# Two layer norms on transposed activations: folding the partial sums on VectorE before the float32 products

## The chip, the cores and the metric

The kernel runs on one core of a Trainium2 chip. The metric is device time of one launch, in microseconds (us). All inputs come from HBM and all outputs go back to it.

## The reference

One inference step of a single-layer encoder on 576 tokens (512 of a prompt, 64 of a sample). The part around the change is the end of the layer:

```python
def layer_norm(x, g, b):
    mu = mean(x, axis=-1);  var = mean(square(x - mu), axis=-1)
    return (x - mu) * rsqrt(var + LN_EPS) * g + b

def finish_layer(x, mix, pe, ...):
    x = layer_norm(ALPHA * x + mix @ w_o, ln1_g, ln1_b)
    hid = square(relu(x @ w_up))                          # 1024 -> 4096
    x = layer_norm(ALPHA * x + hid @ w_down, ln2_g, ln2_b)
    return x + sigmoid(x @ w_ple_gate + b_ple_gate) * (pe @ w_ple)
```

Before it stand a projection of `x` and two kinds of attention, whose outputs make `mix`. Everything is float32.

## The kernel before

Activations lie transposed: the 1024 features are 8 tiles of 128 partitions, the tokens are the columns. `Y` (128 x 8 x 576) holds the residual. The large products split each operand into a high and a low half in a reduced float32 type and make three TensorE products of each pair (`gemm`, L278). The weights are split on the way: ScalarE casts the high half (`whl<-wraw`, L182), VectorE subtracts it for the low half (L186), and SyncE loads the next raw tile into one of a few slots (L163).

A layer norm therefore needs sums over partitions, which TensorE makes with a matrix of 1/1024 (`onesm`). These products are in full float32. The class `LayerNorm` works on one half of the columns: the first norm on A and B of 288 columns each (`L1A`, `L1B`), the second on `A2` of 256 and `B2` of 320 (`L2A`, `L2B`). For each half:

- `add(j)` is called when feature tiles j and j+1 are final. It sums the tiles pairwise into `ln_s` (128 x 2 x w), on VectorE for half A and on GpSimd for the others, the last one (j = 6) always on VectorE (L1103, L1105). After it `ln_s` holds two rows of partial sums.
- `steps()` makes the mean with two products, one for each of the two rows (L1127). It then subtracts the mean on VectorE (L1131), squares on ScalarE (L1133, L1136) and sums the squares, again into two rows (L1137, on VectorE for A and for the last pair, else on GpSimd). The variance comes out of products with `ln_s` as the weights and one column of `onesm`, in blocks of up to 128 tokens, again twice per block (L1145): three blocks for 288 and 320 columns, two for 256. ScalarE takes the root (L1150), VectorE the reciprocal (L1151), and TensorE transposes it back (L64) for the scaling on VectorE (L1160). The high and low halves go to `BH` (ScalarE, L1164) and `BL` (VectorE, L1168).

The first norm runs beside the last two feature tiles of the attention output (`wo2`, whose results VectorE adds to `Y` at L1211) and beside the product with `w_ple` (`ple`, products `g<-pT`, whose results ScalarE copies to `PL` at L1224). Here three PSUM buffers named `g` go round, so that a product group waits until the group three places earlier has been taken out. The second norm runs beside the last `w_down` products (`down_last`, VectorE adds them at L1386) and beside the `w_ple_gate` products.

`drive` walks through a main generator and interleaves the norm's steps with it; `later` puts evictions a step behind. The framework that builds the program may then move an instruction past others of its engine, so that an edit can change the order around it, too. Apart from the sums GpSimd does nothing in this part.

Of the kernel before, what the change touches and what calls it, by code (L numbers as in the profile page):

```python
# [11 lines left out]
OP = mybir.AluOpType  # L12
# [23 lines left out]
def tile_hybrid_step(ctx: ExitStack, tc: tile.TileContext, I, O):  # L36
    nc = tc.nc
    PE, ACT, DVE, POOL, SP = nc.tensor, nc.scalar, nc.vector, nc.gpsimd, nc.sync
# [4 lines left out]
    def f(ap):  # L43
        return ap.bitcast(F32)
# [7 lines left out]
    onesm = base.tile([128, 128], F32, name="onesm")  # L52
# [10 lines left out]
    def transpose(out, in_, n):  # L63
        PE.transpose(out, in_, ident[:n, :n])  # L64
# [58 lines left out]
    class Weights:  # L123
# [9 lines left out]
        def add(self, ap, pool_l=False, pair=None):  # L133
            aps = [ap] if pair is None else [ap, pair]
            n = 2 if pair is None else 7
            self.items.append(dict(aps=aps, h0=self.nh, n=n, pool=pool_l, left=None, when=0))
            self.nh += n
            return len(self.items) - 1
# [941 lines left out]
    def psum_n():  # L1080
        return psN.tile([128, 512], F32, name="n", tag="n", bufs=2)
# [3 lines left out]
    class LayerNorm:  # L1085
# [10 lines left out]
        def add(self, j):  # L1096

            y = Y[:, :, self.sl]
            self.sums = j
            if j == 0:  # L1100
                self.s = fb.tile([128, 2, 320], F32, name="ln_s", tag="ln_s" if self.sl.start else "relu", bufs=1 if self.sl.start else 2)[:, :, :self.w]
            elif j == 2:
                (DVE if self.sl is A else POOL).tensor_tensor(self.s, y[:, 0:2], y[:, 2:4], OP.add)  # L1103
            else:
                (DVE if j == 6 or self.sl is A else POOL).tensor_tensor(self.s, self.s, y[:, j:j + 2], OP.add)  # L1105

        def pump(self):
            return next(self.gen, 0)
# [9 lines left out]
        def steps(self):  # L1118
            sl, gi, w = self.sl, self.gi, self.w
            y = Y[:, :, sl]  # L1120
            while self.sums < 6:
                yield 1
            for _ in range(self.waits[0]):
                yield 1
            mu = psum_n()[:, :w]
            for x in range(2):
                PE.matmul(mu, onesm, self.s[:, x], start=(x == 0), stop=(x == 1))  # L1127
            mb = mu[:, None, :].to_broadcast([128, 2, w])
            ss = self.s
            for j in range(0, 8, 2):  # L1130
                DVE.tensor_tensor(y[:, j:j + 2], y[:, j:j + 2], mb, OP.subtract)  # L1131
                if j == 0:
                    ACT.activation(ss, y[:, 0:2], AF.Square)  # L1133
                else:
                    sq = fb.tile([128, 2, 320], F32, name="ln_sq", bufs=2)[:, :, :w]
                    ACT.activation(sq, y[:, j:j + 2], AF.Square)  # L1136
                    (DVE if j == 6 or sl is A else POOL).tensor_tensor(ss, ss, sq, OP.add)  # L1137
                yield 1
            for _ in range(self.waits[1]):
                yield 1  # L1140
            blks = [(c, min(128, w - c)) for c in range(0, w, 128)]
            var = psum_n()
            for i, (c, n) in enumerate(blks):
                for x in range(2):
                    PE.matmul(var[:n, i:i + 1], ss[:, x, c:c + n], onesm[:, 0:1], start=(x == 0), stop=(x == 1))  # L1145
            rt = fb.tile([128, 4], F32, name="ln_r", bufs=2)
            for i, (c, n) in enumerate(blks):
                if i == 0 or n < 128:
                    m = len(blks) - (blks[-1][1] < 128) if i == 0 else i + 1
                    ACT.activation(rt[:n, i:m], var[:n, i:m], AF.Sqrt, bias=epst[:n, 0:1])  # L1150
                    DVE.reciprocal(rt[:n, i:m], rt[:n, i:m])  # L1151
            for _ in range(self.waits[2]):
                yield 1
            rb = psum_n()[:, :w]
            for i, (c, n) in enumerate(blks):
                transpose(rb[:, c:c + n], rt[:n, i:i + 1].to_broadcast([n, 128]), n)

            def scale(j):
                for x in (j, j + 1):
                    DVE.scalar_tensor_tensor(y[:, x], y[:, x], gb[:, gi, x:x + 1], rb, op0=OP.mult, op1=OP.mult)  # L1160

            def high(j):
                for x in (j, j + 1):
                    ACT.activation(BH[:, x, sl], y[:, x], AF.Identity, bias=gb[:, gi + 1, x:x + 1])  # L1164

            def low(j):
                for x in (j, j + 1):
                    DVE.scalar_tensor_tensor(BL[:, x, sl], y[:, x], gb[:, gi + 1, x:x + 1], f(BH[:, x, sl]),  # L1168
                                             op0=OP.add, op1=OP.subtract)
                self.ready += 1  # L1170

            def bias(j):
                for x in (j, j + 1):
                    ACT.activation(y[:, x], y[:, x], AF.Identity, bias=gb[:, gi + 1, x:x + 1])

            scale(0)
            high(0)
            yield 1
            scale(2)
            high(2)  # L1180
            low(0)
            yield 1
            for j in (4, 6):
                scale(j)
                high(j)
                yield 1
                low(j - 2)
                yield 1
            low(6)
            yield 1  # L1190
            for _ in range(self.waits[3]):
                yield 1
            for j in range(0, 8, 2):
                bias(j)
                yield 1

    def wo2(hs, ln, steps):
        for j in range(0, 8, 2):
            m = psum_g()
            for x in range(2):  # L1200
                cs = slice((j + x) * 128, (j + x + 1) * 128)
                for k in (6, 7):
                    W = unit_w(U["ok", k], U["ok", 6])
                    for _ in gemm(m[:, x, :HW], W, (0,), BH[:, k:k + 1], BL[:, k:k + 1], hs,
                                  first=(k == 6), last=(k == 7), wc=cs):
                        pass
                WT.step(steps)
                yield 1

            def ev(j=j, m=m):  # L1210
                DVE.tensor_tensor(Y[:, j:j + 2, hs], m[:, :, :HW], Y[:, j:j + 2, hs], OP.add)  # L1211
                ln.add(j)
            later(0, ev)
# [95 lines left out]
    def up_sums(g):  # L1309
# [4 lines left out]
        def pair(m):  # L1314
            h0 = WT.items[U["P", g, m]]["h0"]
            r = fs.tile([128, 4, HW], F32, name="r", bufs=2)
            u = fs.tile([128, 3, HW], F32, name="u")
            tt = DVE.tensor_tensor

            steps = ((x11, lambda ps: ACT.copy(u[:, 0], ps)),  # L1320
                     (x12, lambda ps: tt(r[:, 0], ps, u[:, 0], OP.add)),
                     (SX[2], lambda ps: tt(u[:, 1], ps, u[:, 0], OP.add)),  # L1322
                     (SX[3], lambda ps: tt(u[:, 2], ps, u[:, 1], OP.add)),
                     (x22, lambda ps: tt(r[:, 1], ps, u[:, 2], OP.add)),
                     (SX[1], lambda ps: (tt(r[:, 3], ps, u[:, 2], OP.subtract), tt(r[:, 2], ps, u[:, 1], OP.subtract))),
                     (SX[4], lambda ps: tt(r[:, 2], ps, r[:, 2], OP.add)))
            oh, ol = [hid[g][:, x, 2 * m:2 * m + 2].rearrange("p a (b t) -> p (a b) t", b=2) for x in range(2)]
            for i, (x, fn) in enumerate(steps):
                if i % 2 == 0:
                    G = psum_n()[:, None] if i == 6 else psum_g()  # L1330
                ps = G[:, i % 2, :HW]
                hv = WT.half(h0 + i)
                for _ in gemm(ps, lambda part, kw, wc, hv=hv: hv[part][:, kw, wc], range(4), x[0], x[1], slice(0, HW)):
                    WT.step()
                    yield 1
                later(0, lambda fn=fn, ps=ps: fn(ps))
                if i in (4, 6):
                    z = slice(i - 4, i - 2)
                    later(0, lambda z=z: ACT.activation(r[:, z], r[:, z], AF.Relu))
                    later(0, lambda z=z: ACT.activation(r[:, z], r[:, z], AF.Square))  # L1340
                    later(0, lambda z=z: ACT.copy(oh[:, z], r[:, z]))
                    later(0, lambda z=z: tt(ol[:, z], r[:, z], f(oh[:, z]), OP.subtract))
# [213 lines left out]
```

## Time and profile before

| | before |
|---|---|
| time, median of 3 runs | 803.52 us (803.4 to 804.11) |
| profiled execution, span | 802.3 us |
| median above the span | 1.2 us |
| TensorE busy | 788.6 us (98%) |
| VectorE, ScalarE, GpSimd busy | 537.9, 430.5, 118.2 us |
| mean products (L1127) | 16 records |
| variance products (L1145) | 44 records |

The page gives the span of the profiled execution and no other time of it. One float32 product shows as two records, a split product (L278) as one. PE is TensorE, PEld its weight loads, DVE is VectorE, ACT ScalarE, POOL GpSimd, SP SyncE. In a timeline a row gives the start in us, the length of the merged run, the engine, line and operation, the count, and in brackets the idle time before it with what ended it. In the chain, a row gives start, length and what the chain went through.

### The profile page before, as it was taken

The numbers are of one execution on the slowest core, as the hardware profiler recorded it, in microseconds if no ns is written. First come the engines' busy times: TensorE is split into PE (matmuls) and PEld (weight loads), VectorE is DVE, ScalarE is ACT, GpSimd is POOL, SyncE is SP. The second block draws the span as 40 slices with busy tenths as digits, with TensorE's granted clock in tenths as the row PEclk, the third lists the DMA queues.
The fourth block names the chain that finished last, engine by engine and source line by source line (L and its number), as shares of the span: only waits on it lengthen the run. The fifth ranks groups of instructions, "written<-read, shape, count | busy, mean of one in ns | idle before, by whom it ended". The sixth has DMA issues, their size and how long they took to land.

```text
span 802.3 us, 14965 instructions
## 1 busy us (share of the span) xinstructions
PE 788.6 (98%) x5916; PEld 760.0 (95%) x5916; DVE 537.9 (67%) x1092; ACT 430.5 (54%) x904; POOL 118.2 (15%) x117
## 2 busy tenths in 40 slices
PE   7999999999999999999999999999999999999997
PEld 7988898999999999999999999999999999999997
DVE  6679999644456555989755758577594765647553
ACT  5468656787677544497424427154362634626351
POOL 7202344354241000110000000000000000012200
PEclk9999999999999999999999999999999999999999
DMA  8537143254222223442213313142231413720001
GB/s 278 184 42 165 59 111 96 86 183 141 85 86 85 70 81 123 152 152 72 87 53 107 105 53 110 49 132 80 79 106 31 154 54 105 249 106 27 27 28 66
DMA packets 30358, 81.44 MB, mean 102 GB/s; under 512 B 5072, under 2 KB 9168, under 8 KB 30160
## 3 DMA queue, kind: packets, MB, share of 16 engines
q1 hardware_dynamic: 30288, 80.49, 32.3%
q8 instruction: 46, 0.75, 0.4%
q14 instruction: 24, 0.20, 0.1%
HBM read 66.38 MB, written 9.54 MB: 95 GB/s over the span
## 4 chain that ended last, share of the span: by engine, by line
PE 86%; DVE 8%; ACT 2%; DMA 1%; issue 1%; POOL 0%; SPq 0%; DVEq 0%; ACTq 0%
PE g L278 54%; PE m L278 18%; PE n L278 2%; DVE dbias L637 2%; PE V L909 2%; PE T L64 2%; DVE m L635 2%; PE S L822 1%; PE S L423 1%; PE S L820 1%; PE m L416 1%; PE m L423 1%; PE X L64 1%; DVE whl L186 1%; DVE dbias L615 1%
## 5 line engine op out<-in xcount | busy, mean ns | idle before, releaser
L182 ACT CAST whl<-wraw 128x512 fp32r<-128x512 f32 (+1 forms) x226 | 134.9, 611 | 173.4 <-PE g L278 145.6
L278 PE MATMUL g<-BH,whl 128*128 128x288 f32 (+2 forms) x864 | 181.8, 298 | 0.1
L278 PE MATMUL m<-AH,whl 128*128 128x288 f32 x736 | 178.3, 309 | 0.0
L186 DVE TENSOR_TENSOR whl<-wraw,whl 128x512 fp32r<-128x512 f32 (+1 forms) x192 | 129.9, 695 | 69.2 <-ACT whl L182 68.3
L278 PEld LDWEIGHTS g<-BH,whl 128*128 128x128 f32 x864 | 141.2, 188 | 2.3 <-ACT u L1320 1.2
L278 PEld LDWEIGHTS m<-AH,whl 128*128 128x128 f32 x736 | 126.4, 188 | 3.7 <-issue 2.2
L278 PE MATMUL g<-BL,whl 128*128 128x288 f32 (+2 forms) x432 | 127.4, 295 | 0.0
L278 PE MATMUL m<-AL,whl 128*128 128x288 f32 x368 | 109.2, 297 | 0.0
L278 PE MATMUL g<-hidE,whl 128*128 128x288 f32 (+2 forms) x768 | 103.4, 295 | 0.0
L278 PE MATMUL g<-hidO,whl 128*128 128x288 f32 (+2 forms) x768 | 103.3, 295 | 0.0
L278 PEld LDWEIGHTS g<-hidO,whl 128*128 128x128 f32 x768 | 102.3, 188 | 0.0
L278 PEld LDWEIGHTS g<-hidE,whl 128*128 128x128 f32 x768 | 102.2, 188 | 0.1
L278 PEld LDWEIGHTS g<-BL,whl 128*128 128x128 f32 x432 | 81.4, 188 | 0.1
L278 PEld LDWEIGHTS m<-AL,whl 128*128 128x128 f32 x368 | 69.6, 189 | 0.5
L278 PE MATMUL g<-s,whl 128*128 128x288 f32 x432 | 68.5, 298 | 0.0
L278 PEld LDWEIGHTS g<-s,whl 128*128 128x128 f32 x432 | 60.1, 188 | 2.2 <-DVE u L1322 1.1
L838 ACT ACTIVATE sP<-sP,st 128x128 f32<-128x128 f32 (+4 forms) x72 | 39.6, 551 | 40.6 <-DVE st L830 40.2
L1103 POOL TENSOR_TENSOR ln_s<-Y 128x576 f32<-128x576 f32 (+2 forms) x3 | 4.6, 1550 | 383.7 <-DVE Y L1386 371.3
L186 POOL TENSOR_TENSOR whl<-wraw,whl 128x512 fp32r<-128x512 f32 x34 | 44.1, 1297 | 86.8 <-ACT whl L182 68.9
L1361 DVE SCALAR_TENSOR_TENSOR Y<-Y,g 128x576 f32<-128x576 f32 x48 | 36.0, 750 | 21.6 <-PE g L278 21.2
L278 PE MATMUL m<-BH,whl 128*128 128x288 f32 x192 | 43.5, 304 | 0.0
L278 PEld LDWEIGHTS m<-BH,whl 128*128 128x128 f32 x192 | 32.1, 188 | 0.8 <-issue 0.5
(278 smaller groups left out, 1243.2 us busy)
## 6 DMA issues: line engine op xcount, KB each, us to landing
wraw<-in_w_up_dram SPq DMA_DIRECT2D x32, 512.0 KB, 3.5
wraw<-in_w_down_dram SPq DMA_DIRECT2D x32, 512.0 KB, 3.5
wraw<-in_w_qkv_dram SPq DMA_DIRECT2D x23, 512.0 KB, 3.8
wraw<-in_w_gate_dram SPq DMA_DIRECT2D x8, 512.0 KB, 5.0
wraw<-in_w_o_dram SPq DMA_DIRECT2D x8, 384.0 KB, 3.1
out_vT_dram<-v SPq DMA_DIRECT2D x8, 288.0 KB, 2.1
Y<-in_xT_dram SPq DMA_DIRECT2D x8, 288.0 KB, 5.6
PLD<-PL SPq DMA_DIRECT2D x4, 576.0 KB, 2.8
```

Of the source, the lines that this page charges most:

```text
L64: PE.transpose(out, in_, ident[:n, :n])
L182: ACT.copy(self.hv[h][0], src)
L186: eng.tensor_tensor(lv, src, f(hv), OP.subtract)
L278: PE.matmul(ps, W(w, kw, wc), a[:, ka, cols], start=(first and i == 0), stop=(last and i == n - 1))
L416: PE.matmul(mk[:, h, :HW], w0(part, k), a[:, k, h * HW:(h + 1) * HW], start=(k == 0 and i == 0), stop=(k == 7 and i == 2))
L423: PE.matmul(acc[b][:n[b], :304], a[:, k, b * 128:b * 128 + n[b]], ixw(part, k), start=(k == 0 and i == 0), stop=(k == 7 and i == 2))
L615: DVE.scalar_tensor_tensor(dst[:n, :nk], r[:n, :nk], w, dst[:n, :nk], op0=OP.mult, op1=OP.add)
L635: DVE.max(m, s)
L637: DVE.match_replace(out=s, in_to_replace=m, in_values=s, imm_value=GONE)
L838: ACT.activation(j["P"], j["P"], AF.Exp, bias=j["st"][:, 0:1], scale=-1.0, accum_out=s)
L909: PE.matmul(P["O"][r, (i - 1) * 128 + c.start:(i + 1) * 128], P["vt"][:, kb, r], j["PT"][:, hh, kb, c], start=(kb == 0), stop=(kb == i))
L1361: later(0, lambda y=y, m=m, s=s: DVE.scalar_tensor_tensor(y, y, s, m[:, :, :HW], op0=OP.mult, op1=OP.add))
```

## The change

The two rows of partial sums are added into the first by one more VectorE instruction (128 x w), once after the last `add` and once after the last sum of squares. The mean then takes one product and the variance one per block, so that each of the four pairs of the mean and the eleven pairs of the variance loses one product, 15 in all.

```diff
@@ class LayerNorm, add
                 (DVE if j == 6 or self.sl is A else POOL).tensor_tensor(self.s, self.s, y[:, j:j + 2], OP.add)
+            if j == 6:
+                DVE.tensor_tensor(self.s[:, 0], self.s[:, 0], self.s[:, 1], OP.add)
@@ steps
             mu = psum_n()[:, :w]
-            for x in range(2):
-                PE.matmul(mu, onesm, self.s[:, x], start=(x == 0), stop=(x == 1))
+            PE.matmul(mu, onesm, self.s[:, 0], start=True, stop=True)
...
                     (DVE if j == 6 or sl is A else POOL).tensor_tensor(ss, ss, sq, OP.add)
+                if j == 6:
+                    DVE.tensor_tensor(ss[:, 0], ss[:, 0], ss[:, 1], OP.add)
                 yield 1
...
             for i, (c, n) in enumerate(blks):
-                for x in range(2):
-                    PE.matmul(var[:n, i:i + 1], ss[:, x, c:c + n], onesm[:, 0:1], start=(x == 0), stop=(x == 1))
+                PE.matmul(var[:n, i:i + 1], ss[:, 0, c:c + n], onesm[:, 0:1], start=True, stop=True)
```

In the changed kernel the new additions are L1107 (sum) and L1140 (squares); L1128 is the mean, L1147 the variance, L1132 the subtraction, L1138 the sum of squares, L1213 the addition of `wo2`, L1226 the copy to `PL`. In the second norm the built program has the same order as before with the new instructions put in. In the first norm three engines run in another order.

VectorE, from the addition of tiles 2 and 3 of half B (`Y<-g,Y`) on; before:

```order
L1211 TENSOR_TENSOR Y<-g,Y 128x2x288
L186 TENSOR_TENSOR whl<-wraw,whl 128x512
L1131 TENSOR_TENSOR Y<-Y,n 128x2x288 x2
L1211 TENSOR_TENSOR Y<-g,Y 128x2x288
L1131 TENSOR_TENSOR Y<-Y,n 128x2x288
L1137 TENSOR_TENSOR ln_s<-ln_s,ln_sq 128x2x288
L1131 TENSOR_TENSOR Y<-Y,n 128x2x288
L1137 TENSOR_TENSOR ln_s<-ln_s,ln_sq 128x2x288
L1211 TENSOR_TENSOR Y<-g,Y 128x2x288
L1137 TENSOR_TENSOR ln_s<-ln_s,ln_sq 128x2x288
L1105 TENSOR_TENSOR ln_s<-ln_s,Y 128x2x288
```

The same stretch of VectorE in the changed kernel:

```order
L1213 TENSOR_TENSOR Y<-g,Y 128x2x288
L1107 TENSOR_TENSOR ln_s<-ln_s 128x288
L186 TENSOR_TENSOR whl<-wraw,whl 128x512
L1213 TENSOR_TENSOR Y<-g,Y 128x2x288
L1132 TENSOR_TENSOR Y<-Y,n 128x2x288 x4
L1138 TENSOR_TENSOR ln_s<-ln_s,ln_sq 128x2x288
L1213 TENSOR_TENSOR Y<-g,Y 128x2x288
L1138 TENSOR_TENSOR ln_s<-ln_s,ln_sq 128x2x288
L1105 TENSOR_TENSOR ln_s<-ln_s,Y 128x2x288
L1138 TENSOR_TENSOR ln_s<-ln_s,ln_sq 128x2x288
L1107 TENSOR_TENSOR ln_s<-ln_s 128x288
L1140 TENSOR_TENSOR ln_s<-ln_s 128x288
```

The four subtractions now stand in one block behind the third `Y<-g,Y` of half B, and the fourth comes behind one sum of squares where two stood before.

ScalarE over the squares of half A; before (with what each instruction waits for):

```order
L182 CAST whl<-wraw 128x512 [waits DMAHW1_49,PE_49]
L1133 ACTIVATE ln_s<-Y 128x2x288 [waits DVE_49]
L1136 ACTIVATE ln_sq<-Y 128x2x288 [waits DVE_49]
L182 CAST whl<-wraw 128x512 [waits PE_49]
L182 CAST whl<-wraw 128x512 [waits DMAHW2_49,PE_49]
L1136 ACTIVATE ln_sq<-Y 128x2x288 [waits DVE_49]
L1224 COPY PL<-g 128x576 [waits PE_49]
```

The same stretch of ScalarE in the changed kernel:

```order
L182 CAST whl<-wraw 128x512 [waits PE_49]
L1134 ACTIVATE ln_s<-Y 128x2x288 [waits DVE_49]
L182 CAST whl<-wraw 128x512 [waits DMAHW2_49,PE_49]
L1137 ACTIVATE ln_sq<-Y 128x2x288 [waits DVE_49] x2
L1226 COPY PL<-g 128x576 [waits PE_49]
```

A weight cast moved ahead of the first square; the first copy to `PL` stays behind the two squares into `ln_sq`.

TensorE at the second mean, after the first 12 `g<-pT` products; before:

```order
L278 MATMUL g<-pT,whl 128x288 [waits DVE_49]
L278 MATMUL g<-pT,whl 128x288 x11
L278 MATMUL g<-pT,whl 128x288 [waits Activation_49]
L278 MATMUL g<-pT,whl 128x288 x2
L278 MATMUL g<-pT,whl 128x288 [waits DVE_49]
L278 MATMUL g<-pT,whl 128x288 x9
L1127 MATMUL n<-ln_s,onesm 128x288 [waits DVE_49]
L1127 MATMUL n<-ln_s,onesm 128x288
```

The same stretch of TensorE in the changed kernel:

```order
L278 MATMUL g<-pT,whl 128x288 [waits DVE_49]
L278 MATMUL g<-pT,whl 128x288 x11
L278 MATMUL g<-pT,whl 128x288 [waits Activation_49]
L278 MATMUL g<-pT,whl 128x288 x4
L278 MATMUL g<-pT,whl 128x288 [waits DVE_49]
L278 MATMUL g<-pT,whl 128x288 x16
L1128 MATMUL n<-ln_s,onesm 128x288 [waits DVE_49]
L1147 MATMUL n<-onesm,ln_s 128x1 [waits DVE_49]
```

The second mean (half B) stands nine split products later than before, with the first variance (half A) right behind it. The first mean, too, stands eight split products later than before, in the last group of `wo2`. The second variance keeps its place behind the last `g<-pT` product, and the second set of transposes stands 46 split products behind it where 42 stood.

On SyncE the second of two `w_up` loads now comes behind three stores of `PL` instead of ahead of them.

## The prediction

> **What bounds the kernel now.** I read the page first (busy shares, then the chain that ended last), then the chain cut to the two norms, then the waits and the timelines of each engine there.
>
> ```profile
> span 802.3 us, 14965 instructions
> PE 788.6 (98%) x5916; PEld 760.0 (95%) x5916; DVE 537.9 (67%) x1092; ACT 430.5 (54%) x904; POOL 118.2 (15%) x117
> PE 86%; DVE 8%; ACT 2%; DMA 1%; issue 1%; POOL 0%; SPq 0%; DVEq 0%; ACTq 0%
> ```
>
> TensorE is the bound: what leaves its queue leaves the time, unless a wait takes its place. The chain in the first norm (300 to 350 us) and the second (715 to 765 us) has every product group that the change halves:
>
> ```profile
> 327.57 0.99 PE n L1127 x4
> 336.52 0.98 PE n L1127 x4
> 337.77 1.00 PE n L1145 x12
> 347.52 1.00 PE n L1145 x12
> 718.02 0.86 PE n L1127 x4
> 731.21 0.79 PE n L1145 x8
> 748.76 1.08 PE n L1127 x4
> 760.59 1.11 PE n L1145 x12
> ```
>
> All eight lie on the chain. Together they are 0.99 + 0.98 + 0.86 + 1.08 = 3.91 us for the mean and 1.00 + 1.00 + 0.79 + 1.11 = 3.90 us for the variance.
>
> The two norms differ in what stands beside them. Busy time by stretch, then VectorE and GpSimd in the first norm:
>
> ```profile
> 318.00:330.00 12.00, 11.86 (x85) 11.20 (x84) 11.93 (x20) 5.92 (x10) 1.78 (x1) 1.00 0.57 190
> 327.17 0.75 DVE L1211 TENSOR_TENSOR Y<-g,Y 128x576 f32<-128x576 f32 x1
> 327.83 0.68 DVE L186 TENSOR_TENSOR whl<-wraw,whl 128x512 fp32r<-128x512 f32 x1
> 328.58 1.42 DVE L1131 TENSOR_TENSOR Y<-Y,n 128x576 f32<-128x576 f32 x2
> 331.25 1.63 DVE L1137 TENSOR_TENSOR ln_s<-ln_s,ln_sq 128x576 f32<-128x576 f32 x1
> 334.13 0.74 DVE L1211 TENSOR_TENSOR Y<-g,Y 128x576 f32<-128x576 f32 x1
> 328.05 1.78 POOL L1103 TENSOR_TENSOR ln_s<-Y 128x576 f32<-128x576 f32 x1 [12.39 <-DVE Y L1211]
> 330.81 1.45 POOL L1105 TENSOR_TENSOR ln_s<-ln_s,Y 128x576 f32<-128x576 f32 x1 [0.98 <-DVE Y L1211]
> ```
>
> In the first row VectorE (fourth figure) is busy 11.93 of 12.00 us, while TensorE (second figure) is busy 11.86. So in the first norm two engines are full, and an instruction added to VectorE is not free there.
>
> **The products removed.** Is half of the records half of the time? The mean of 256, 288 and 320 columns takes 0.86, 0.99 and 1.08 us, which is 3.36, 3.44 and 3.38 ns per column: the time goes with the columns and has no fixed part that would stay. The variance takes 0.79 / 8 = 0.099 us per record of a full block. So the saving is 3.91 / 2 = 1.95 us and 3.90 / 2 = 1.95 us: 1.92 us of the sum in the second norm, 1.98 us in the first. From below, a switch that stays at 0.1 us for each of the eight groups would leave 3.1 us; I take 3.9 because of the three widths.
>
> **The additions, second norm.** Four additions, of 256 and 320 columns. Their cover:
>
> ```profile
> 714.46 0.69 DVE L1105 TENSOR_TENSOR ln_s<-ln_s,Y 128x512 f32<-128x512 f32 x1
> 724.08 0.69 DVE L1137 TENSOR_TENSOR ln_s<-ln_s,ln_sq 128x512 f32<-128x512 f32 x1 [1.20 <-POOL ln_s L1137]
> 745.37 0.83 DVE L1105 TENSOR_TENSOR ln_s<-ln_s,Y 128x640 f32<-128x640 f32 x1
> 755.59 0.83 DVE L1137 TENSOR_TENSOR ln_s<-ln_s,ln_sq 128x640 f32<-128x640 f32 x1 [2.70 <-POOL ln_s L1137]
> ```
>
> The sums end at 715.15, 724.8, 746.2 and 756.4; by the chain rows the products that need them take their turn at 718.02, 731.21, 748.76 and 760.59. The smallest distance is 2.6 us. An addition there costs at most 0.83 us (the row of twice its width), so all four are covered by queued split products, even if TensorE comes 0.4 to 1.4 us earlier. Behind them on VectorE wait weight halves and, last, the gate's output for half A2; VectorE has idle time in brackets in two of these rows, so nothing late reaches TensorE. Cost 0; second norm -1.92 us.
>
> **The additions, first norm.** Four additions of 128x288 from SBUF, a form that the trace does not have. Neighbours:
>
> ```profile
> 351.47 3.07 DVE L186 TENSOR_TENSOR whl<-wraw,whl 128x512 fp32r<-128x512 f32 x5
> L1326 DVE TENSOR_TENSOR r<-n,r x12: 448/452/458, 439.2 to 691.6; 128x288 f32<-128x288 f32 x12
> ```
>
> Back to back, 576 columns are spaced 0.66 us (327.17 to 327.83) and 512 columns (3.07 - 0.68) / 4 = 0.60 us, about 1.04 ns per column; that puts 288 columns at 0.37 us of queue. The other end is the full length of 0.45 us with one operand in PSUM. I take 0.37, since the queue is packed there. The Trainium skill, VectorE: DVE Perf Modes, section "The DRAIN you can't avoid", says that the next op does not start before the pipe is empty, which would charge the full length; here L186 starts at 327.83, 0.09 us before the L1211 in front of it ends, so the trace disagrees. By the rule the four would take 1.8 us instead of 1.5 us.
>
> More costly is whom the first addition lets in. It stands at 327.83 in front of the weight half L186 that stood there, and GpSimd asks for its sum at 328.05:
>
> ```profile
> 721.02 3.03 POOL L1137 TENSOR_TENSOR ln_s<-ln_s,ln_sq 128x512 f32<-128x512 f32 x2 [8.11 <-ACT ln_sq L1136]
> 721.48 1.40 DVE L186 TENSOR_TENSOR whl<-wraw,whl 128x512 fp32r<-128x512 f32 x1
> ```
>
> A VectorE addition with both operands in SBUF that meets a running GpSimd sum takes 1.40 instead of 0.69 us and ends after it (also 331.25: 1.63 us instead of 0.75), while the subtraction at 328.58, with one operand in PSUM, ran at normal speed beside the sum at 328.05. The Trainium skill, SBUF — State Buffer, section "SBUF: two separate sides", calls this an exclusive lock that goes to whichever starts first, for its whole instruction; these rows agree, and who gets it between two VectorE instructions in a row the rule leaves open (rival b).
>
> Before, L186 was first and GpSimd waited (1.78 against 1.45 us). Now the addition ends at 328.20, GpSimd runs to about 329.65, and L186 goes with it to about 330.1, 1.6 us later than before. The queue then runs: third `Y<-g,Y` to 330.8, four subtractions to 333.4, one sum of squares to 334.1, fourth `Y<-g,Y` to 334.8. ScalarE follows the subtractions: square, cast, two squares to 333.85, first copy to `PL` to 334.4. TensorE waits for these:
>
> ```profile
> 327.40 1.14 PE L1127 MATMUL n<-ln_s,onesm 128*128 128x288 f32 x4
> 330.79 3.74 PE L278 MATMUL g<-pT,whl 128*128 128x288 f32 x27
> 334.93 1.59 PE L278 MATMUL g<-pT,whl 128*128 128x288 f32 x10 [0.40 <-DVE Y L1211]
> 332.58 0.64 ACT L1224 COPY PL<-g 128x576 f32<-128x576 f32 x1 [0.24 <-PE g L278]
> 344.64 0.76 DVE L1137 TENSOR_TENSOR ln_s<-ln_s,ln_sq 128x576 f32<-128x576 f32 x1 [1.89 <-POOL ln_s L1137]
> 345.66 1.86 PE L278 MATMUL g<-pT,whl 128*128 128x288 f32 x12 [0.15 <-ACT PL L1224]
> 351.33 0.20 DVE L1151 RECIPROCAL ln_r<-ln_r 128x2 f32<-128x2 f32 x2
> 354.25 0.39 PE n L64 x3
> ```
>
> One split product takes (3.74 - 0.29) / 26 = 0.133 us. In my working the mean starts at 327.40 + 8 x 0.133 = 328.47 (its addition is done by 328.2) and takes 0.49; the `g<-pT` products start at 330.29. After 24 of them, at 333.47, the next group needs the buffer that the first `PL` copy frees at 334.4: a wait of about 1.0 us, where before 0.55 us passed between 334.38 and 334.93 for the fourth `Y<-g,Y`. Then 5 and 17 products bring the second mean to 337.36, with its sum done by 337.3. Before it stood at 336.36, nine products earlier, so TensorE is 9 x 0.133 - 1.0 = 0.2 us ahead: of the 0.49 saved, 0.3 went into the longer wait. Second mean and first variance give 0.99 more: 1.2 us ahead.
>
> Next is the second variance, at 347.52 before. Behind the wait for `PL` that ended at 345.66, TensorE could now be there at 337.36 + 0.98 + 50 x 0.133 + 0.45 = 345.45, since a copy to `PL` moved ahead. But GpSimd's two sums of squares end about where they did, L1137 of half B starts near 344.4, a scaling (0.43) and the new addition follow (0.37), so the variance starts at about 346.0: 1.5 us ahead, and 2.0 us after its own halving. The transposes follow 46 products later, at 352.6. Their reciprocals stood at 351.33, with almost 3 us to spare before 354.25; now two weight halves (0.60 each) and the addition stand ahead of them, to about 352.4. That cover is nearly gone; I charge 0.1 us, with 0 to 0.5 as bounds. After that TensorE is packed and the order around it free by microseconds; the `w_up` load behind the `PL` stores leaves at about 348, for a weight not needed for over 15 us. First norm: -1.9 us.
>
> **Sum.** -1.92 - 1.9 = -3.8 us, against the profiled span 802.3 (1.2 us under the median, an offset I keep): 803.5 - 3.8 = 799.7 us. A measurement of this kernel can tell about 0.2%, 1.6 us, from no change.
>
> **Rivals.** (a) The first norm gives back all it saves: VectorE is full there, and the wait at 333.47 grows by another 1.9 us. For it: 11.93 of 12.00 us busy. Against it: the added queue time is 1.5 us and only partly before the waits. Left is the second norm: 803.5 - 1.9 = 801.6; a little more loss and it is no change (to 801.9 and above).
>
> (b) No block: VectorE's L186 gets in ahead of GpSimd as it does now, and the fourth `Y<-g,Y` comes 1.3 us before 334.8. Then there is no wait at 333.47, the old 0.55 goes, and so does the one before 345.66 (0.39): -1.98 - 0.94 = -2.9 in the first norm, 803.5 - 4.8 = 798.7, and 798.2 if TensorE's smaller waits there go with them. For it: L186 now follows its predecessor without a gap; against it: at 741.26 GpSimd came in between three such.
>
> ```profile
> 741.26 3.27 DVE L186 TENSOR_TENSOR whl<-wraw,whl 128x512 fp32r<-128x512 f32 x3
> ```
>
> Three take 3 x 0.60 + 0.09 = 1.9 us alone.
>
> (c) Slower: the blocking repeats. GpSimd has four sums in the first norm, two of them here:
>
> ```profile
> 341.66 2.95 POOL L1137 TENSOR_TENSOR ln_s<-ln_s,ln_sq 128x576 f32<-128x576 f32 x2 [9.40 <-ACT ln_sq L1136]
> ```
>
> If each holds up one VectorE instruction for its 1.45 us in the path of a TensorE wait, and the additions cost their 1.5 us, that is +7.3 - 3.9: 806.9. It decides from 5.5 us of new waits on. Against it: in the new order the second to fourth sums run beside subtractions and scalings, which have a PSUM operand.
>
> (d) The change saves less than half of the product time: if the variance were fixed per block, 803.5 - 1.85 = 801.6. The three widths speak for the mean; for the variance, 12 records with a narrow last block take less than 12 / 8 of 0.79.
>
> **Chances.** The forecast (798.9 to 800.9) 0.53; (b) 0.12; (a) and (d) with 801 to 801.9 0.17, above that 0.11; (c) and other mishaps 0.07. Faster 0.53 + 0.12 + 0.17 = 0.82, same 0.11, slower 0.07. The range from 798.2 to 801.7 leaves out the last two cases and little else.
>
> **What would show it.** Right: 8 records on the mean's line and 22 on the variance's, each group half as long; in the second norm no TensorE wait; in the first norm L186 after the first new addition at about 1.8 us, a TensorE wait of about 1 us for the first `PL` copy, and almost none at the second transposes. Wrong: groups longer than half, waits of over 2 us in all in the first norm, or a wait on the new additions.

## The result, and the profile after

| | before | after |
|---|---|---|
| time, median of 4 runs | 803.63 us (803.4 to 804.11) | 799.16 us (798.7 to 799.83) |
| ratio of the times | | 0.9946, 95% interval 0.9934 to 0.9957 |
| span of the profiled execution | 802.3 us | 797.2 us |
| TensorE busy | 788.6 us | 783.8 us |

The change saves 4.5 us, 0.54%. The forecast was 799.7 us.

From the page after (busy time, then the shares of the chain that ended last): TensorE is still the bound, and VectorE has only 1.5 us more work.

```profile
PE 783.8 (98%) x5886; PEld 755.7 (95%) x5886; DVE 539.4 (68%) x1100; ACT 430.3 (54%) x904; POOL 119.0 (15%) x117
PE 87%; DVE 8%; ACT 2%; DMA 1%; issue 1%; POOL 0%; SPq 0%; DVEq 0%; ACTq 0%
```

The chain of the changed kernel (start, length, what it went through), at the mean and variance groups that it passes; in the fence the mean is L1128 and the variance L1147:

```profile
328.09 0.48 PE n L1128 x2
336.18 0.50 PE n L1128 x2
344.62 0.76 PE n L1147 x6
351.63 0.39 PE n L64 x3
714.89 0.43 PE n L1128 x2
727.64 0.34 PE n L1147 x4
744.75 0.54 PE n L1128 x2
756.05 0.54 PE n L1147 x6
```

Against 0.99, 0.98, 0.86 and 1.08 us the four means now take 0.48, 0.50, 0.43 and 0.54; the variances of the second norm take 0.34 and 0.54 against 0.79 and 1.11. The product time does halve. (The row of 0.76 us at 344.62 comes straight behind a wait, which comes up below.)

To see which norm gained what, I cut each run at one point that it has in its chain before the first norm and one between the norms. Before first, then after:

```profile
321.44 1.85 PE g L278 x12
...
432.52 2.38 PE g L278 x16
```
```profile
320.89 1.84 PE g L278 x12
...
429.37 2.39 PE g L278 x16
```

| stretch | before | after | difference | forecast |
|---|---|---|---|---|
| to the start of the x12 row | 321.44 | 320.89 | -0.55 | 0 |
| first norm, to the start of the x16 row | 432.52 - 321.44 = 111.08 | 108.48 | -2.60 | -1.9 |
| second norm, to the end of the span | 802.3 - 432.52 = 369.78 | 367.83 | -1.95 | -1.92 |

The first line is not put down to the change, since at the same cut the other kernels below start between 320.34 and 321.38, and it is part of why the profiled spans differ by 5.1 us where the medians differ by 4.5. The second norm came as forecast. The first gained 0.7 us more than forecast.

TensorE's waits there, as its weight loads (PEld) show them between 319 and 360 us (engine and line, what it waited for, us in total, times, longest us; the waits of the transposes, for no engine, are the same in both and left out). Before, then after:

```profile
PEld g L278 <- DVE Y L1211: 1.2, 3, 0.6
PEld g L278 <- ACT PL L1224: 0.4, 1, 0.4
```
```profile
PEld g L278 <- DVE Y L1213: 0.6, 2, 0.3
PEld n L1147 <- DVE ln_s L1140: 0.3, 1, 0.3
```

The prediction had a wait of 1.0 us for the first `PL` copy. It isn't there; the old wait of 0.6 for the fourth `Y<-g,Y` and the 0.4 for `PL` are gone, and one of 0.3, on the new addition of squares, has come. With 1.98 us of products and 1.6 - 0.9 = 0.7 us of waits, the sum is -2.7, against -2.6 measured.

VectorE and GpSimd in the first norm after (rows between them left out) show what became of the expected block:

```profile
327.28 0.45 DVE L1107 TENSOR_TENSOR ln_s<-ln_s 128x288 f32<-128x288 f32 x1
327.65 0.68 DVE L186 TENSOR_TENSOR whl<-wraw,whl 128x512 fp32r<-128x512 f32 x1
328.25 0.75 DVE L1213 TENSOR_TENSOR Y<-g,Y 128x576 f32<-128x576 f32 x1
328.92 2.74 DVE L1132 TENSOR_TENSOR Y<-Y,n 128x576 f32<-128x576 f32 x4
331.88 0.76 DVE L1138 TENSOR_TENSOR ln_s<-ln_s,ln_sq 128x576 f32<-128x576 f32 x1 [0.23 <-ACT ln_sq L1137]
332.55 0.75 DVE L1213 TENSOR_TENSOR Y<-g,Y 128x576 f32<-128x576 f32 x1
335.22 0.45 DVE L1107 TENSOR_TENSOR ln_s<-ln_s 128x288 f32<-128x288 f32 x1
335.59 0.45 DVE L1140 TENSOR_TENSOR ln_s<-ln_s 128x288 f32<-128x288 f32 x1
327.50 2.15 POOL L1103 TENSOR_TENSOR ln_s<-Y 128x576 f32<-128x576 f32 x1 [12.38 <-DVE Y L1213]
329.72 1.46 POOL L1105 TENSOR_TENSOR ln_s<-ln_s,Y 128x576 f32<-128x576 f32 x1
```

GpSimd asked for its sum at 327.50, in the middle of the new addition. The weight half L186 followed the addition at 327.65 and took its normal 0.68 us, and GpSimd's sum took 2.15 us where it takes 1.46 alone. So VectorE did not wait for GpSimd; GpSimd waited, through two instructions instead of one (1.78 us before). The fourth `Y<-g,Y` starts 11.66 us after the cut (332.55 - 320.89), against 12.69 before: 1.03 us earlier, although VectorE has one addition more ahead of it. Most of that, 0.87 us, is a block of before that is gone. There the first sum of squares met GpSimd's second sum and took 1.63 us (the prediction's row at 331.25). After, GpSimd's second sum (329.72 to 331.18) runs beside the four subtractions, which have an operand in PSUM, and the sum of squares at 331.88 takes 0.76. That the weight half gets in first, with no wait at the first `PL` copy, is rival (b).

### The profile page after: what moved, and what is told of

Same layout as the page of the kernel before. It is cut to its first block, busy times and chain, and to the rows that moved or that the text cites. A ratio compares the mean times of both kernels' runs of the same rounds, so it can differ in the third digit from the quotient of the medians.

```text
span 797.2 us, 14908 instructions
## 1 busy us (share of the span) xinstructions
PE 783.8 (98%) x5886; PEld 755.7 (95%) x5886; DVE 539.4 (68%) x1100; ACT 430.3 (54%) x904; POOL 119.0 (15%) x117
## 4 chain that ended last, share of the span: by engine, by line
PE 87%; DVE 8%; ACT 2%; DMA 1%; issue 1%; POOL 0%; SPq 0%; DVEq 0%; ACTq 0%
PE g L278 55%; PE m L278 18%; PE n L278 2%; DVE dbias L637 2%; PE V L909 2%; PE T L64 2%; DVE m L635 2%; PE S L822 1%; PE S L820 1%; PE m L416 1%; PE S L423 1%; PE X L64 1%; PE m L423 1%; DVE whl L186 1%; DVE dbias L615 1%
## 5 line engine op out<-in xcount | busy, mean ns | idle before, releaser
L186 DVE TENSOR_TENSOR whl<-wraw,whl 128x512 fp32r<-128x512 f32 (+1 forms) x192 | 130.0, 696 | 66.1 <-ACT whl L182 65.2
L186 POOL TENSOR_TENSOR whl<-wraw,whl 128x512 fp32r<-128x512 f32 x34 | 44.1, 1297 | 86.8 <-ACT whl L182 68.9
```

The costliest lines, as they stand in the source:

```text
L186: eng.tensor_tensor(lv, src, f(hv), OP.subtract)
```

## Experiments

Two theories after the result. **Order:** in the first norm the additions cost TensorE nothing, and the order in which VectorE's queue now stands takes away 0.7 us of waits; everything else is products. **Rival, price:** the halved products save more than their records show (by their stationary loads, or by the switch to another kind of product), and the additions take some of it back.

All times below are medians (of 5 runs for e1 and e4, 7 for e2, 11 for e5, 10 for e3 and 4 for e6), with the kernel before at 803.67 us (17 runs) beside e1, e2, e4 and e5, and at 803.51 us (13 runs) beside e3 and e6. Their lines shift by a few; the mean, the variance and the additions are named in words. The 95% intervals reach 0.7 to 1.3 us to each side, so two accounts half a microsecond apart are told apart by the chain of one profiled execution each, not by the medians. How well such a stretch repeats shows in e3: its first norm has the program of before and takes 111.09 us against 111.08.

### e1: the mean's half alone

```diff
 steps (against the changed kernel)
-                if j == 6:
-                    DVE.tensor_tensor(ss[:, 0], ss[:, 0], ss[:, 1], OP.add)
...
-                PE.matmul(var[:n, i:i + 1], ss[:, 0, c:c + n], onesm[:, 0:1], start=True, stop=True)
+                for x in range(2):
+                    PE.matmul(var[:n, i:i + 1], ss[:, x, c:c + n], onesm[:, 0:1], start=(x == 0), stop=(x == 1))
```

> Only the sums are folded (four additions, four products of the mean fewer); the variance keeps its two products per block. VectorE's order in the first norm is that of the changed kernel. Theory (products plus a wait that the new order takes away): second norm -0.97 us (half of 0.86 + 1.08), first norm -0.98 for the products and about -0.6 because the block of four subtractions brings the fourth addition to Y forward, in all -2.5 us. Rival (the first norm's extra gain came with the halved variance): first norm -1.0, in all -2.0 us.

Measured: 800.71 us, ratio 0.9961 (0.9948 to 0.9975), -2.96 us. The cut rows of its chain, and its only wait on VectorE or ScalarE between 319 and 360 us:

```profile
320.81 1.85 PE g L278 x12
...
430.08 2.38 PE g L278 x16
```
```profile
PEld g L278 <- DVE Y L1212: 0.6, 2, 0.3
```

First norm 430.08 - 320.81 = 109.27, so -1.81: 0.99 of products and 1.0 of waits that are gone (1.6 to 0.6) would make -2.0. The mean's half of the change alone brings the new order of VectorE, and with it the gain from the waits. (The median alone would allow the rival's -2.0 us, too: the interval is -4.2 to -2.0.)

### e2: the variance's half alone

```diff
 add, steps (against the changed kernel)
-            if j == 6:
-                DVE.tensor_tensor(self.s[:, 0], self.s[:, 0], self.s[:, 1], OP.add)
...
-            PE.matmul(mu, onesm, self.s[:, 0], start=True, stop=True)
+            for x in range(2):
+                PE.matmul(mu, onesm, self.s[:, x], start=(x == 0), stop=(x == 1))
```

> Only the sums of squares are folded (four additions, eleven products of the variance fewer); the mean keeps its two products. VectorE's order in the first norm is nearly that of before. Theory: second norm -0.95 us, first norm -1.0 us with the old TensorE waits (0.4 to 0.6 us each) still there, in all -1.95 us. Rival (the extra gain came with the halved variance): first norm -1.6, in all -2.6 us.

Measured: 801.57 us, ratio 0.9973 (0.9962 to 0.9984), -2.10 us. Its chain and its waits, in the same views:

```profile
320.34 1.85 PE g L278 x12
...
430.40 2.38 PE g L278 x16
```
```profile
PEld g L278 <- DVE Y L1212: 1.2, 3, 0.6
PEld g L278 <- ACT PL L1225: 0.4, 1, 0.4
```

First norm 110.06, so -1.02; the waits are those of before, and the products (1.00 of 2.00) are all that was gained. e1 and e2 make -5.06 together, 0.6 more than the whole change. By the cuts their first norms add up to -2.83 against -2.60; the 0.3 us wait for the addition of squares, which only the whole change has, is of this size. The other 0.4 us is less than the intervals can tell.

### e4: the products halved, no additions

```diff
 add and steps (against the changed kernel)
-            if j == 6:
-                DVE.tensor_tensor(self.s[:, 0], self.s[:, 0], self.s[:, 1], OP.add)
...
-                if j == 6:
-                    DVE.tensor_tensor(ss[:, 0], ss[:, 0], ss[:, 1], OP.add)
```

> The 15 products are taken out and the eight additions are not put in, so the second row of the partial sums is left out of the mean and the variance. VectorE's order in the first norm is nearly that of before. Theory (the additions cost nothing, the order takes away the waits): second norm -1.92 us as in the changed kernel, first norm -2.0 us with the old wait for the fourth addition to Y grown by the 0.49 us that TensorE comes earlier, so -1.5 to -2.0: in all -3.4 to -3.9 us, not faster than the changed kernel. Rival (the additions cost their VectorE time in the full first norm): 1.5 us faster than the changed kernel, in all -6.0 us.

Measured: 799.61 us, ratio 0.9947 (0.9934 to 0.9959), -4.06 us. Without its eight additions the kernel is not faster than with them (0.9946). Chain and waits:

```profile
321.38 1.85 PE g L278 x12
...
430.47 2.38 PE g L278 x16
```
```profile
PEld g L278 <- DVE Y L1209: 1.0, 3, 0.4
PEld n L1143 <- DVE ln_s L1136: 0.6, 1, 0.6
```

First norm 109.09, so -1.99: the 1.98 us of products, with 1.6 us of waits in all, as before. They lie elsewhere in part: the one for the `PL` copy is gone, and TensorE waits for the sum of squares of half B instead. This is the price of the products by itself, and it is the one that the records gave: the rival on price falls.

### e5: the additions, with all the old products

```diff
 steps (against the changed kernel)
-            PE.matmul(mu, onesm, self.s[:, 0], start=True, stop=True)
+            for x in range(2):
+                PE.matmul(mu, onesm, self.s[:, x], start=(x == 0), stop=(x == 1))
...
-                PE.matmul(var[:n, i:i + 1], ss[:, 0, c:c + n], onesm[:, 0:1], start=True, stop=True)
+                for x in range(2):
+                    PE.matmul(var[:n, i:i + 1], ss[:, x, c:c + n], onesm[:, 0:1], start=(x == 0), stop=(x == 1))
```

> The eight additions are put in and all products are kept as before, so the second row counts twice. VectorE's order in the first norm is that of the changed kernel. Theory: second norm 0.0 us, first norm -0.3 to -0.7 us, since the new order takes away a TensorE wait and the additions lie beside products: in all -0.3 to -0.7 us against before. Rival (the additions cost their VectorE time where that engine is full): +1.5 us.

Measured: 803.60 us, ratio 0.9999 (0.999 to 1.0008), -0.07 us. Chain and waits:

```profile
320.69 1.85 PE g L278 x12
...
431.60 2.38 PE g L278 x16
```
```profile
PEld g L278 <- ACT PL L1228: 0.9, 1, 0.9
PEld g L278 <- DVE Y L1215: 0.6, 2, 0.3
```

First norm 110.91, so -0.17; second 801.4 - 431.60 = 369.8, nothing. Eight additions cost nothing in either norm. The 0.6 us wait for the fourth `Y<-g,Y` is gone here too, but the `PL` wait is 0.9 instead of 0.4: TensorE came earlier to the next thing that it had to wait for. That is less than the -0.3 to -0.7 us expected for the first norm: in these runs the order saves its 0.7 to 1.0 us of waits only where products are halved as well.

### e3: the change in the second norm alone

```diff
 add and steps (against the changed kernel)
-            if j == 6:
+            if j == 6 and self.gi == 2:
...
+            nx = 1 if gi == 2 else 2
+            for x in range(nx):
+                PE.matmul(mu, onesm, self.s[:, x], start=(x == 0), stop=(x == nx - 1))
... (the variance in the same way)
```

> Only the second norm is folded; the program of the first norm is that of before, instruction by instruction. Theory: second norm -1.92 us (half of 0.86 + 0.79 + 1.08 + 1.11), first norm 0.0, in all -1.9 us. Rival (part of the second norm's gain is the first norm's order coming down later): second norm less than -1.5 us.

Measured: 801.71 us, ratio 0.9977 (0.9968 to 0.9986), -1.80 us. By its chain the first norm is unchanged (432.42 - 321.33 = 111.09) and the second takes 800.5 - 432.42 = 368.08, so -1.7:

```profile
321.33 1.84 PE g L278 x12
...
432.42 2.39 PE g L278 x16
```

The four additions of the second norm are covered, as forecast.

### e6: GpSimd asks just before an addition ends

The block that the prediction expected might depend on when GpSimd asks. Here one more VectorE instruction of 128 x 200 from SBUF stands ahead of the addition for half A (its result isn't used), and L186 and the next `Y<-g,Y` are held in the order that the changed kernel has.

```diff
 (against the changed kernel)
-                eng.tensor_tensor(lv, src, f(hv), OP.subtract)
+                self.last = eng.tensor_tensor(lv, src, f(hv), OP.subtract)
...
             if j == 6:
+                if self.sl is A:
+                    extra = fb.tile([128, 200], F32, name="extra")
+                    DVE.tensor_tensor(extra, self.s[:, 0, :200], self.s[:, 1, :200], OP.add)
...
-                DVE.tensor_tensor(Y[:, j:j + 2, hs], m[:, :, :HW], Y[:, j:j + 2, hs], OP.add)
+                with (tc.issue_after(WT.last.ins) if hs is B and j == 4 else ExitStack()):
+                    DVE.tensor_tensor(Y[:, j:j + 2, hs], m[:, :, :HW], Y[:, j:j + 2, hs], OP.add)
```

> The changed kernel with one more VectorE addition of 128x200 (its result is not used) ahead of the first new addition, and the third addition of half B to Y held behind the weight half, so that VectorE runs: second addition to Y of half B, extra addition, weight half, new addition, third addition to Y. The new addition then comes about 0.65 us after the start of GpSimd's sum, where in the changed kernel the weight half came 0.15 us after it and was not held up. Theory (GpSimd takes the port between two VectorE instructions in a row if its start lies far enough ahead, between 0.15 and 0.37 us by the rows so far): the weight half takes 0.7 us, the new addition about 1.6 instead of 0.45 us, TensorE waits about 1 us for it in front of the first mean, and the first norm gains 1.2 to 1.6 instead of 2.6 us against before. Rival (VectorE keeps the port as long as its instructions follow each other without a gap): the new addition takes 0.45 us, no TensorE wait there, the first norm gains 2.2 to 2.6 us.

Measured: 798.90 us, ratio 0.9944 (0.9928 to 0.9961), -4.61 us, the changed kernel's own gain. The timelines of VectorE and GpSimd there:

```profile
327.31 0.35 DVE L1109 TENSOR_TENSOR extra<-ln_s 128x200 f32<-128x200 f32 x1
327.59 0.68 DVE L186 TENSOR_TENSOR whl<-wraw,whl 128x512 fp32r<-128x512 f32 x1
328.19 0.45 DVE L1110 TENSOR_TENSOR ln_s<-ln_s 128x288 f32<-128x288 f32 x1
328.56 0.75 DVE L1217 TENSOR_TENSOR Y<-g,Y 128x576 f32<-128x576 f32 x1
327.53 2.40 POOL L1103 TENSOR_TENSOR ln_s<-Y 128x576 f32<-128x576 f32 x1 [12.38 <-DVE Y L1217]
```

L186 came between the two, so the addition itself was now the one that GpSimd's request, at 327.53, should have held up. It took 0.45 us. GpSimd's sum took 2.40 us: it waited through three VectorE instructions from SBUF. The theory that GpSimd gets in at the next gap fell here in both forms, the prediction's and this one; that such instructions in a row keep it out held here (the last section has a row where it did not).

TensorE's waits between 319 and 360 us are 0.6 us in all, since the 0.3 on the addition of squares is missing, and the first norm is shorter by as much. The first point behind it that both chains have, after first, then e6:

```profile
431.76 1.19 PE n L278 x9
```
```profile
PEld g L278 <- DVE Y L1217: 0.6, 2, 0.3
...
431.51 1.19 PE n L278 x9
```

From the first cut (320.92 in e6) this is 431.51 - 320.92 = 110.59 us, against 431.76 - 320.89 = 110.87 after and 434.90 - 321.44 = 113.46 before: -2.87 for e6, with 1.98 of products and 1.0 of waits. By the second norm's first mean the 0.28 us are lost again (the row behind it starts 394.43 us after the first cut in both), at a place that I have not found.

## Why the prediction was right, and where it was off

The total was right: 799.7 forecast, 799.16 measured, inside the range of 798.2 to 801.7. But 799.16 lies as near to rival (b)'s 798.7, so the time alone chooses neither account; the profile does, and in the first norm it chooses (b). Step by step:

- **Products removed, 3.9 us.** Right. e4 shows -1.99 in the first norm, 798.2 - 430.47 = 367.73 or -2.05 in the second, and -4.06 in all; the widths gave the price, and nothing of it stays as a fixed part. Rival (d) is out.
- **Additions of the second norm, nothing.** Right: e3 gives -1.80 and after -1.95, for 1.92. No wait of TensorE on them.
- **Queue time of an addition, 0.37 us.** Right to the hundredth: 327.28 to 327.65, and 335.22, 335.59, 335.96 (where L186 starts). Their own length is 0.45. The Trainium skill, VectorE: DVE Perf Modes, section "The DRAIN you can't avoid", has the next operation start once the pipe is empty, unless nothing holds it, and these are the second kind: in each of the three places the next starts 0.08 us before the one in front of it ends. The prediction left that exception out when it said that the trace disagrees.
- **The failed step: "Now the addition ends at 328.20, GpSimd runs to about 329.65, and L186 goes with it to about 330.1".** GpSimd did not get in between. L186 took 0.68 us instead of the forecast 1.8, and the wait of 1.0 us at 333.47 did not come. So the mis-sized term is the first norm, -1.9 forecast and -2.60 measured. Rival (b) had it, at -2.9 for this norm and 798.7 in all; I had given it 0.12. What (b) lacked is the 0.3 us wait for the new addition of squares: e6, without it, gains 2.87.
- **Why the old wait went, too.** The prediction saw that the four subtractions go in one block, but priced only the loss. With L186 unhindered, the fourth `Y<-g,Y` comes 1.03 us earlier: it stands ahead of a second sum of squares that had stood before it, and the first one no longer meets a GpSimd sum. All eight profiles agree. In the old order (before, e2, e3, e4) that sum of squares took 1.63, 1.63, 1.64 and 1.38 us, and TensorE's longest wait for the `Y<-g,Y` was 0.4 to 0.7 us; in the new order (after, e1, e5, e6) it took 0.75 or 0.76 and the wait is gone. That the order is the cause, and not the additions that came with it, was not tried by itself: no run gave the kernel before the new order alone.
- **Second variance at 346.0, behind GpSimd's chain.** The mechanism was right: it stands behind GpSimd's two sums, a sum of squares, a scaling and the new addition. The chain after has them one behind the other, up to the variance at 344.62 (two short rows of "issue" left out):

```profile
341.55 1.43 POOL ln_s L1138
343.01 0.76 DVE ln_s L1138
343.77 0.42 DVE Y L1162
344.19 0.38 DVE ln_s L1140
```

  TensorE's weight loads waited 0.3 us for L1140, and the variance behind them takes 0.76 us, where the same six records take 0.54 at 756.05. It came at 344.62, 1.4 us earlier than said, since everything ahead of it came earlier.
- **Transposes with almost no slack.** Wrong, in the kernel's favour: the reciprocals stood at 350.81 instead of near 352.4, the transposes at 351.63, and the only wait charged to them is 0.2 us for no engine, as before.

```profile
350.81 0.20 DVE L1153 RECIPROCAL ln_r<-ln_r 128x2 f32<-128x2 f32 x2
```

- **Rival (c), GpSimd blocking over and over,** is out for the first norm. In the second, where the prediction saw it before, it is there again in after, and TensorE has no wait from it.

## What to carry to other kernels

Where TensorE is the bound and VectorE's queue has cover, trading float32 products for VectorE additions can pay the products' full time (here 3.9 us), with the additions free as long as no TensorE wait hangs on them: price the removed records first, and then look for the one new wait. An added instruction also moves the order of its queue, and the move can matter more than the instruction (here 0.7 us of waits went, while the 4 x 0.37 us of queue cost nothing that shows in the time), so compare the waits before and after, not only the busy time. Price a possible block of one engine by another from both sides: the chance for either outcome should have been nearer to even, since the trace before had a row for each.

## What the runs showed of the hardware

In the first norm a GpSimd sum that asked while VectorE ran instructions with both operands in SBUF waited for all of them in a row, not only for the one it met: of 1.46 us alone, it took 1.78 (one left to wait for), 2.15 (the rest of one, and one) and 2.40 us (the rest of one, and two), and counted back from its end by those 1.45 us, it began each time about when the next VectorE instruction, with an operand in PSUM, did (329.65 - 1.45 = 328.20 after, 329.93 - 1.45 = 328.48 in e6). The Trainium skill, SBUF — State Buffer, section "SBUF: two separate sides", calls the port an exclusive lock for the whole of an instruction; these runs agree that GpSimd waits, and add who comes next in these three cases. One row goes the other way. In the second norm after, VectorE and GpSimd:

```profile
737.25 3.27 DVE L186 TENSOR_TENSOR whl<-wraw,whl 128x512 fp32r<-128x512 f32 x3
737.48 1.89 POOL L1105 TENSOR_TENSOR ln_s<-ln_s,Y 128x640 f32<-128x640 f32 x1 [6.02 <-DVE Y L1388]
```

Three weight halves take 1.9 us alone and took 3.27; GpSimd asked 0.23 us into the first and came in behind it. Both cases have VectorE instructions from SBUF in a row, and what makes the difference is open: the request came 0.15 us before the next VectorE instruction started after, 0.37 us before it here, and 0.06 and 0.66 us before the two that passed in e6, so how far ahead it comes does not decide it.
